# Tile addresses in multiples of 128 bytes, and the second block's first norm applied behind its projections

## The chip, the cores and the metric

The kernel runs on one core of a Trainium2 chip. The metric is the time of one execution on the device in microseconds (us); the median of three runs before the change is 2263.63 us. A core has TensorE (PE in the profile; its weight loads are listed apart as PEld), VectorE (DVE), ScalarE (ACT), GpSimd (POOL) and SyncE (SP); POOL, SP and ACT also issue DMAs here. On-chip memory (SBUF) has 128 partitions; a tile of 128x1024 fp32 takes 4096 bytes of each, and its address is the byte at which it starts in every partition.

## The reference

256 tokens of width 1024, fp32, go through two layers with PEER (a dense evaluation of 16,384 experts per layer here) and then a second block with attention, a linear recurrence (RG-LRU) and an MLP. Shortened:

```
for layer in (0, 1):                       # first block
    mix = diff_attention(x) if layer == 0 else stick_breaking(x)
    x = layer_norm(ALPHA * x + mix, ln_g[layer, 0], ln_b[layer, 0])
    x = layer_norm(ALPHA * x + peer(x), ln_g[layer, 1], ln_b[layer, 1])

u = x * rsqrt(mean(x * x, -1) + 1e-6) * attn_pre_norm        # second block
q, k, v, x_lru, g_lru, gate_attn, gate_lru = split(u @ w_in)
y_attn = moba_attention(rope(q), rope(k), v) @ w_branch_attn
y_lru = (rg_lru(conv(x_lru)) * gelu(g_lru)) @ w_branch_lru
mix = (sigmoid(gate_attn) * y_attn + sigmoid(gate_lru) * y_lru) @ w_out
h = x + rms_norm(mix)
h = h + rms_norm(square(relu(rms_norm(h) @ w_mlp_up)) @ w_mlp_down)
```

The factor of the rms norm is one number per token, so it can be taken out of the product: (r * x * gain) @ w is r * ((x * gain) @ w).

## The kernel before

Weights come as 740 tiles of 128x1024 fp32 in the order of `plan`. SyncE's queue loads them into a ring of four `raw` tiles (L50). `Stream.split` makes two fp32r tiles of each: `hi`, a cast on ScalarE (L66), and `lo = raw - hi` on VectorE (L67). Splits run two tiles ahead of the tile in use, within three pairs of `hi` and `lo`; tiles named in `keep` have buffers of their own. x is kept transposed in the same two parts, `xh` and `xl`, written by `transposed` (four TensorE transposes into PSUM, L300, then a cast, L163, and a subtraction, L164). Each product is three fp32r matmuls, high by high, high by low, low by high (L157 to L159 in `mm3`, L182 in `mm_n`).

There are two shapes of matmul. `proj_t` holds the weight tile stationary and streams 256 tokens of `xh` or `xl` (256 columns); it serves PEER's up product, the first block's q and k, the second block's x_lru, g_lru and gates, and the MLP's up product. `proj_half`, `half_pass` and `mm_n` hold 128 tokens of x (or of a hidden activation: `wh` and `wo` in PEER's down product, `uh` and `ul` in the MLP's, `mh` and `ml` in w_out) stationary and stream 512 columns of the weight tile. In a row such as `ps_h<-xh,hi` the moving operand stands first, the stationary one behind it. `ah`, `ch`, `lrr` and `laa` are activations of the second block in proj_t's role or of the recurrence's gates.

TensorE's instructions are issued in program order; while one matmul runs, the stationary operand of the next is loaded (PEld). Each engine works through its own queue in the order in which the code was written; `bg.tick()` lets background generators issue a piece of their work between tiles.

The junction from PEER to what follows: the last six weight tiles of PEER's down product are held back for the second token half (`held`, run by `finish`), so that the layer norm of the first 128 tokens (`b` = 0) runs beside them. `layer_norm` then does, per token half: the norm (`norm`, L316 to L329, on VectorE with two small ScalarE steps L266, L267 for the root), the transposes, and `half_pass(b)`, the product of this token half with the first four kept weight tiles (512 columns of the first projection). At the end of PEER 1 a pre-norm lies between norm and transposes:

```
after(b):  pre_norm(x[:, b], gain)      # before; result pnu
    squares of both halves and their sum: ACT L933 x2, DVE L935
    u[:, half] = x[:, half] * gain       # DVE L946, L948
    r = rsqrt(...)                       # ACT L266, L267, DVE L268 to L273
    u[:, :512] *= r (DVE L950); u[:, 512:] *= r (ACT L951)
```

After the junction come five calls of `proj_half` of four tiles each (the second half of q, then k and v; rope on q and k runs on VectorE behind each), then the `proj_t` products of x_lru, the two gates and, later, g_lru.

SBUF pools lie one behind another from the left and from the right; every tile is padded to a multiple of 32 bytes. Small tiles (two `eps` of 4 bytes, `gcol`, `factor`) therefore shift what follows. Addresses modulo 256, before and after (from the built programs):

```
tile                          before   after
xh, xl, jd                       128     128
raw, hi, lo (the ring's)         192     128
wh, wo (PEER down)               192     128
uh, ul (MLP down)                224       0
mh, ml (w_out)                   224       0
ah, al (branch product)           32     128
lrr, laa (recurrence gates)      224       0
x2x, x2gains (new)                 -     128
```

Full-size matmuls (fp32r, 256 or 512 columns) in the program, by the address of the moving operand less that of the next matmul's stationary operand, modulo 256:

```
columns  before                                                     after
256      192: 8294  96: 299  32: 191  others 48                     0: 8620  128: 204  64: 8
512      0: 3279  64: 473  224: 340  96: 234  128: 72  others 65    0: 3996  128: 467
```

Of the kernel before, what the change touches and what calls it, by code (L numbers as in the profile page):

```python
# [9 lines left out]
F32 = mybir.dt.float32  # L10
# [115 lines left out]
class Kernel:  # L126
    def __init__(self, tc, ctx, a):
# [85 lines left out]

    def proj_half(self, xh, xl, dst, banks="h"):
# [24 lines left out]

    def half_pass(self, b, tiles):  # L240

# [13 lines left out]
        if b:  # L255
            for i, ps in enumerate(self.passed):
                self.nc.scalar.copy(self.jd[:, i, :512], ps)
            self.passed = []
# [46 lines left out]

    def norm(self, pool, b, acc, x, g, beta):

# [18 lines left out]
        for s in halves:  # L326
            if s is halves[1]:
                centre(s)
            nc.vector.scalar_tensor_tensor(x[:, b, s], y[:, s], r, beta[:, s], ALU.mult, ALU.add)  # L329
        yield  # L330

    def layer_norm(self, pool, acc, x, g, beta, after=None):


        tiles = []
        for _ in self.norm(pool, 0, acc[0], x, g, beta):
            pass
        u0 = after(0) if after else x[:, 0]
        n1 = self.norm(pool, 1, acc[1], x, g, beta)
# [40 lines left out]
    def layer0(self, pool_x):  # L380
        nc, tc, a = self.nc, self.tc, self.a
        with ExitStack() as ctx:
# [24 lines left out]
            nc.sync.dma_start(lp.rearrange("p a b -> p (a b)"), a["lam"].unsqueeze(0).to_broadcast([P, 256]))  # L407
            gcol = one.tile([P, 1], F32, tag="gcol", name="gcol0")
            nc.sync.dma_start(gcol, a["subln"])
# [236 lines left out]
    def peer(self, layer, spill, begin):  # L646
# [212 lines left out]
        with ExitStack() as ctx:  # L859
# [58 lines left out]
            tp = ctx.enter_context(tc.tile_pool(name=f"n{layer}", bufs=1, reuse_waits="tile"))  # L918
            self.layer_norm(tp, acc, xr, gb, bb, extra(tp, xr) if extra else None)
            nc.gpsimd.dma_start(spill, xr)  # L920
# [16 lines left out]

    def pre_norm(self, pool, x, gain):

        nc = self.nc  # L940
        r = pool.tile([P, 1], F32, tag="pn_r", name=f"pnr{self.n}", bufs=2)
        u = pool.tile([P, D], F32, tag="ln_y", name=f"pnu{self.n}", bufs=2)
        halves = [slice(0, 512), slice(512, D)]
        root = self.mean_square(pool, r, [x[:, s] for s in halves], 1e-6)
        next(root)
        nc.vector.tensor_tensor(u[:, halves[0]], x[:, halves[0]], gain[:, halves[0]], ALU.mult)  # L946
        next(root)
        nc.vector.tensor_tensor(u[:, halves[1]], x[:, halves[1]], gain[:, halves[1]], ALU.mult)  # L948
        next(root)
        nc.vector.tensor_scalar(u[:, halves[0]], u[:, halves[0]], r, None, ALU.mult)  # L950
        nc.scalar.mul(u[:, halves[1]], u[:, halves[1]], r)  # L951
        return u

    def late_norm(self, pool, x, square):

        r = pool.tile([P, 1], F32, tag="lt_r", name=f"ltr{self.n}", bufs=2)
        yield from self.mean_square(pool, r, [x[:, :512], x[:, 512:]], 1e-6)
# [42 lines left out]
    def block2(self, spill):  # L1000
# [3 lines left out]
        fp = ctx_f.enter_context(tc.tile_pool(name="b2f", bufs=1))  # L1004
        factor = fp.tile([P, NB], F32, tag="factor", name="factor")
        keep = outer.enter_context(tc.tile_pool(name="b2o", bufs=1))
        with ExitStack() as ctx:
# [11 lines left out]
            nc.gpsimd.dma_start(cv, a["cols2"])  # L1019
            gb = one.tile([P, KD, 2], F32, tag="gb", name="gb2")  # L1020
# [4 lines left out]
            qk = [self.jd, kn]  # L1025
            v = keep.tile([P, NB, D], F32, tag="vh", name="v2")
            ah = one.tile([P, KD, T], F32R, tag="ah", name="ah2")
# [132 lines left out]
            def project(dst, c):  # L1160
                nc.scalar.copy(dst[:, c], self.proj_t(self.xh, self.xl))

            for dst in (qk[0], qk[1], v):
                for half in range(2):
                    if half or dst is not qk[0]:
                        self.proj_half(self.xh, self.xl, dst[:, :, half * 512 : half * 512 + 512], "acc")
                    if dst is not v:
                        rope(dst, half)
            self.bg.add(heads())
            self.bg.add(lru())  # L1170
            for half in range(2):
                ch = one.tile([P, 4, T], F32R, tag="ch", name=f"ch{half}")
                cl = one.tile([P, 4, T], F32R, tag="cl", name=f"cl{half}")
                for j in range(4):
                    c = half * 4 + j
                    o = self.proj_t(self.xh, self.xl)
                    xp = two.tile([P, T + 3], F32, tag="xp", name=f"xp{c}")
# [7 lines left out]
                    for dst in (ga, gl):  # L1185
                        nc.scalar.activation(dst[:, c], self.proj_t(self.xh, self.xl), AF.Tanh, scale=0.5)
                        if dst is ga:
# [31 lines left out]
            self.bg.drain()  # L1219
            xp = outer.enter_context(tc.tile_pool(name="b2x", bufs=1, side="right"))  # L1220
            x = xp.tile([P, NB, D], F32, tag="x", name="x2")
            nc.gpsimd.dma_start(x, spill)
            gains = self.gains(xp, "gains", a["attn_post_norm_2"][0], a["mlp_pre_norm_2"][0])
            mh = keep.tile([P, KD, T], F32R, tag="vh", name="mh2")
# [68 lines left out]
def body(tc, a, stop="all"):  # L1293
    nc = tc.nc
    with ExitStack() as ctx:
# [18 lines left out]
        def begin(pool, late):  # L1314
            (pre,) = k.gains(pool, "pre", a["attn_pre_norm_2"][0], late=late)
            return lambda temps, x: lambda b: k.pre_norm(temps, x[:, b], pre)

# [87 lines left out]
```

## Time and profile before

| | |
|---|---|
| median of 3 runs | 2263.63 us (2262.33 to 2263.73) |
| profiled execution | 2266.94 us |
| its span | 2265.1 us |
| mean granted TensorE clock | 0.994 |

All rows shown come from this one profiled execution. A row of the timeline has the start in us from the span's start, the duration, engine, line, operation, out<-in, shapes, the count of merged instructions and, in brackets, the idle time before it with what ended it. A row of the windows has the stretch, its length, for each engine the busy time and the number of instructions, the granted clock (1.00 is full speed), the share of the DMA engines and GB/s. A matmul's duration overlaps its successors' (0.28 us for 256 columns, 0.39 for 512, while a new one starts every 0.11 or 0.23 us), so pace is read from starts or from counts.

### The profile page before, as it was taken

What the parts mean: (1) busy time and instruction counts of PE and PEld (TensorE: products, weight loads), DVE (VectorE), ACT (ScalarE), POOL (GpSimd) and SP (SyncE); (2) the same over time, 40 slices, a digit from 0 to 9 for tenths busy, and PEclk for the clock granted to TensorE, in tenths of its full rate; (3) what the DMA queues carried; (4) which work ended last, traced back from release to release, by engine and by line L of the source; (5) the groups of instructions that cost most, each with busy time, mean ns of one, the idle gap of its engine ahead of it and who ended that gap; (6) DMA issues with size and microseconds to landing.
All of it is one profiled execution on the core that took longest, in us unless ns stands there. A gap on an engine that the chain in (4) does not pass through costs nothing.

```text
span 2265.1 us, 39924 instructions
## 1 busy us (share of the span) xinstructions
PE 2218.6 (98%) x15028; PEld 2002.1 (88%) x15028; DVE 1757.5 (78%) x3501; ACT 1229.2 (54%) x2115; POOL 54.8 (2%) x118
## 2 busy tenths in 40 slices
PE   8999999999999999999999999999999899999998
PEld 7779999999888887988999999988888789997986
DVE  6879998887776668677999888777666857886754
ACT  5744455666544554674445566644554546655643
POOL 4200000000000000000000000000000000000000
PEclk9999999999999999999999999999999999999999
DMA  7556676557777777545666655777777655555664
GB/s 247 160 175 230 218 233 228 195 202 239 253 242 242 243 238 248 191 138 178 224 226 233 221 199 194 264 243 243 239 244 258 211 176 165 177 175 179 214 187 139
DMA packets 151954, 481.96 MB, mean 213 GB/s; under 512 B 17888, under 2 KB 18944, under 8 KB 150480
## 3 DMA queue, kind: packets, MB, share of 16 engines
q1 hardware_dynamic: 126576, 423.09, 58.2%
q10 hardware_dynamic: 19008, 34.61, 4.1%
q0 software_dynamic: 6176, 21.70, 2.7%
q8 instruction: 118, 1.93, 0.3%
q14 instruction: 76, 0.62, 0.1%
HBM read 437.39 MB, written 39.85 MB: 211 GB/s over the span
## 4 chain that ended last, share of the span: by engine, by line
PE 84%; DVE 6%; issue 4%; ACT 3%; DMA 3%; POOL 0%; ACTq 0%; DVEq 0%; SPq 0%; POOLq 0%
PE ps_acc L182 31%; PE ps_h L157 15%; PE ps_h L159 15%; PE ps_h L158 15%; DVE lo L67 1%; PE ps_acc L821 1%; PE ps_acc L822 1%; PE ps_acc L158 1%; PE ps_acc L157 1%; PE ps_acc L159 1%; ACT hi L66 1%; PE ps_acc L705 0%; DMA raw<-peer_w_q 0%; DMA raw<-peer_v 0%; DVE lns L319 0%
## 5 line engine op out<-in xcount | busy, mean ns | idle before, releaser
L67 DVE TENSOR_TENSOR lo<-raw,hi 128x1024 fp32r<-128x1024 f32 x740 | 901.5, 1222 | 414.3 <-ACT hi L66 410.8
L66 ACT CAST hi<-raw 128x1024 fp32r<-128x1024 f32 x740 | 774.6, 1050 | 432.6 <-issue 288.0
L157 PE MATMUL ps_h<-xh,hi 128*128 128x256 f32 x2784 | 789.9, 284 | 0.8 <-ACT k L628 0.8
L159 PE MATMUL ps_h<-xh,lo 128*128 128x256 f32 x2784 | 774.5, 278 | 3.4 <-DVE lo L67 3.3
L158 PE MATMUL ps_h<-xl,hi 128*128 128x256 f32 x2784 | 774.4, 278 | 0.0
L157 PEld LDWEIGHTS ps_h<-xh,hi 128*128 128x128 f32 x2784 | 526.3, 189 | 5.9 <-issue 1.7
L159 PEld LDWEIGHTS ps_h<-xh,lo 128*128 128x128 f32 x2784 | 525.1, 189 | 4.2 <-DVE lo L67 4.2
L158 PEld LDWEIGHTS ps_h<-xl,hi 128*128 128x128 f32 x2784 | 524.7, 188 | 0.2
L182 PE MATMUL ps_acc<-hi,wh 128*128 128x512 f32 x1024 | 317.9, 390 | 0.1
L182 PE MATMUL ps_acc<-hi,wo 128*128 128x512 f32 x1024 | 318.0, 390 | 0.0
L182 PE MATMUL ps_acc<-lo,wh 128*128 128x512 f32 x1024 | 317.4, 389 | 0.2 <-DVE lo L67 0.2
L848 ACT ACTIVATE hs<-ps_h 128x256 f32<-128x256 f32 x254 | 97.6, 384 | 341.0 <-PE ps_h L159 171.6
L182 PEld LDWEIGHTS ps_acc<-hi,wh 128*128 128x128 f32 x1024 | 191.6, 188 | 41.8 <-ACT wh L163 2.4
L182 PEld LDWEIGHTS ps_acc<-hi,wo 128*128 128x128 f32 x1024 | 191.8, 188 | 41.1 <-DVE wo L164 1.6
L182 PEld LDWEIGHTS ps_acc<-lo,wh 128*128 128x128 f32 x1024 | 192.1, 188 | 40.5 <-DVE lo L67 0.7
L874 DVE TENSOR_TENSOR jd<-G,jd 128x256 f32<-128x256 f32 x256 | 106.9, 418 | 3.3 <-ACT G L824 3.3
L164 DVE TENSOR_TENSOR wo<-jd,wh 128x256 fp32r<-128x256 f32 x256 | 107.2, 419 | 2.0 <-ACT wh L163 2.0
L163 ACT CAST wh<-jd 128x256 fp32r<-128x256 f32 x256 | 101.7, 397 | 10.0 <-DVE jd L874 9.8
L824 ACT ACTIVATE G<-ps_acc 128x64 f32<-128x64 f32 (+1 forms) x256 | 81.9, 385 | 7.4 <-issue 1.5
L157 PE MATMUL ps_h<-hi,xh 128*128 128x512 f32 x160 | 68.4, 428 | 9.0 <-ACT hi L66 8.0
L821 PE MATMUL ps_acc<-oh 128*128 128x128 f16 x512 | 69.4, 221 | 0.0
L822 PE MATMUL ps_acc<-oh 128*128 128x128 f16 x512 | 68.3, 219 | 0.0
(359 smaller groups left out, 2372.7 us busy)
## 6 DMA issues: line engine op xcount, KB each, us to landing
raw<-peer_u SPq DMA_DIRECT2D x256, 512.0 KB, 4.5
raw<-peer_v SPq DMA_DIRECT2D x256, 512.0 KB, 4.3
jd<-H ACTq DMA_DIRECT2D x128, 256.0 KB, 4.2
H<-hs SPq DMA_DIRECT2D x126, 256.0 KB, 2.1
raw<-w_in SPq DMA_DIRECT2D x32, 512.0 KB, 3.7
raw<-w_up SPq DMA_DIRECT2D x32, 512.0 KB, 4.0
raw<-w_down SPq DMA_DIRECT2D x32, 512.0 KB, 3.7
raw<-w_qkv SPq DMA_DIRECT2D x24, 512.0 KB, 4.4
```

What stands on the lines that cost most here:

```text
L66: self.nc.scalar.copy(hi, raw)
L67: self.nc.vector.tensor_sub(lo, raw, hi)
L157: mm(out, lh, rh, start=start, stop=False)
L158: mm(out, lh, rl, start=False, stop=False)
L159: mm(out, ll, rh, start=False, stop=stop)
L163: self.nc.scalar.copy(hi, src)
L164: self.nc.vector.tensor_sub(lo, src, hi)
L182: mm(acc[half], x, w[:, half * 512 : half * 512 + 512], start=a, stop=b)
L821: mm(out, o[:, 0, j], o[:, 1, j], start=True, stop=False)
L822: mm(out, o[:, 0, j], o[:, 2, j], start=False, stop=True)
L848: nc.scalar.activation(hs[i // 2][:, i % 2], o, AF.Gelu)
L874: nc.vector.tensor_tensor(w, g[:, i - first], hl[i // 2][:, i % 2], ALU.mult)
```

## The change

Two things in one diff.

Pads. `factor` and `gcol` are widened to 128 and 64 bytes, `gb` to 128; two unused tiles, of 64 bytes behind the constants on the left and 96 on the right, bring what follows to multiples of 128 bytes (table above). No instruction belongs to this.

The late factor. `pre_norm` is gone. `norm` takes a function `then` that multiplies each half of x by the gain, into the norm's own buffer `lny`, directly behind the norm of that half (L355), and the transposes read it. The rms factor of each token half is computed by `late_factor` (squares, sum and root as before) into `self.factor`, and enters where products leave PSUM with tokens on partitions: in `half_pass` (L268) and `proj_half` (L237), as a multiply on ScalarE in place of the copy. The `proj_t` products have tokens along the free dimension, so x is rescaled for them: the factor goes through DRAM (`rd`) and comes back spread over all partitions (`rb`), and the background generator `rescale` does `xz = (xh + xl) * rb` and splits it into `x2`, a pair of k at a time, over eight ticks that begin after eleven. `x2` takes 16 KB on the right, later reused for `x` and `gains`.

```diff
+        self.factor = c.tile([P, 32], F32, tag="factor", name="fac")[:, :NB]
         self.ident = c.tile([P, P], F32, tag="ident", name="ident")
+        pads = {"left": 64, "right": 96}
+        c.tile([P, pads["left"] // 4], F32, tag="pad", name="padl")
+        top = ctx.enter_context(tc.tile_pool(name="top", bufs=1, side="right"))
+        top.tile([P, pads["right"] // 4], F32, tag="pad", name="padr")
...
     def proj_half(self, xh, xl, dst, banks="h", by=None):
-            self.nc.scalar.copy(dst[:, b], acc[b])
+            if by is None:
+                self.nc.scalar.copy(dst[:, b], acc[b])
+            else:
+                self.nc.scalar.mul(dst[:, b], acc[b], by[:, b : b + 1])
...
     def norm(self, pool, b, acc, x, g, beta, then=None):
             nc.vector.scalar_tensor_tensor(x[:, b, s], y[:, s], r, beta[:, s], ALU.mult, ALU.add)
+            if then:
+                then(y, s)
...
+    def layer_norm(self, pool, acc, x, g, beta, gain=None):
+            def scaled(b):
+                def then(y, s):
+                    u[b] = y
+                    nc.vector.tensor_tensor(y[:, s], x[:, b, s], gain[:, s], ALU.mult)
+                return then
+            factors = [self.late_factor(pool, x[:, b], self.factor[:, b : b + 1]) for b in range(NB)]
...
         for h in range(2):
             next(n1)
-            self.transposed(0, h, u0)
+            self.transposed(0, h, u[0])
         self.st.split(self.st.used + NJ, self.st.used)
+        if factors:
+            next(factors[0])
         next(n1)
         self.half_pass(0, tiles)
-        u1 = after(1) if after else x[:, 1]
         for h in range(2):
-            self.transposed(1, h, u1)
-        self.half_pass(1, tiles)
+            self.transposed(1, h, u[1])
+        if factors:
+            next(factors[1])
+            for f in factors:
+                for _ in f:
+                    pass
+        self.half_pass(1, tiles, self.factor if factors else None)
...
+    def late_factor(self, pool, x, r):
+        yield from self.mean_square(pool, r, [x[:, :512], x[:, 512:]], 1e-6)
...
+            x2 = [rx.tile([P, KD, T], F32R, tag=t, name="x2" + t) for t in ("x", "gains")]
+            nc.gpsimd.dma_start(rd.rearrange("b p -> p b"), self.factor)
+            nc.gpsimd.dma_start(rb, rd.rearrange("b p -> (b p)").unsqueeze(0).to_broadcast([P, T]))
+            def rescale():
+                for _ in range(11):
+                    yield
+                for k in range(0, KD, 2):
+                    s = slice(k, k + 2)
+                    z = two.tile([P, 2, T], F32, tag="m2", name=f"xz{k}")
+                    nc.vector.tensor_tensor(z, self.xh[:, s].bitcast(F32), self.xl[:, s].bitcast(F32), ALU.add)
+                    yield
+                    nc.vector.tensor_tensor(z, z, rb.unsqueeze(1).to_broadcast([P, 2, T]), ALU.mult)
+                    self.part(x2[0][:, s], x2[1][:, s], z)
+                    yield
...
-                        self.proj_half(self.xh, self.xl, dst[:, :, half * 512 : half * 512 + 512], "acc")
+                        self.proj_half(self.xh, self.xl, dst[:, :, half * 512 : half * 512 + 512], "acc", self.factor)
-                    o = self.proj_t(self.xh, self.xl)
+                    o = self.proj_t(*x2)
```

TensorE's order keeps its 15,708 rows; only names change. On VectorE, the norm of the first 128 tokens at the end of PEER 1 (`xr` is the normed x, `pnu` before and `lny` after what the transposes read), before:

```order
L329 SCALAR_TENSOR_TENSOR xr_19679<-lny_21198,lnr_21201,gains_20816 128x512
L323 SCALAR_TENSOR_TENSOR lny_21198<-lny_21198,lnm_21200,gains_20816 128x512
L329 SCALAR_TENSOR_TENSOR xr_19679<-lny_21198,lnr_21201,gains_20816 128x512
L946 TENSOR_TENSOR pnu_21221<-xr_19679,gains_20817 128x512
L935 TENSOR_TENSOR mss_21223<-mss_21223 128x1
L268 TENSOR_SCALAR rsx_21228<-mss_21223 128x1
L948 TENSOR_TENSOR pnu_21221<-xr_19679,gains_20817 128x512
L270 SCALAR_TENSOR_TENSOR rsz_21230<-rsy_21229,rsx_21228 128x1
L271 TENSOR_SCALAR rsz_21230<-rsz_21230 128x1
L273 TENSOR_TENSOR pnr_21220<-rsy_21229,rsz_21230 128x1
L950 TENSOR_SCALAR pnu_21221<-pnu_21221,pnr_21220 128x512
L316 SCALAR_TENSOR_TENSOR lny_21240<-xr_19679,ps_acc_18173 128x512
```

The same place after:

```order
L340 SCALAR_TENSOR_TENSOR xr_19685<-lny_21204,lnr_21207,gains_20822 128x512
L355 TENSOR_TENSOR lny_21204<-xr_19685,gains_20823 128x512
L334 SCALAR_TENSOR_TENSOR lny_21204<-lny_21204,lnm_21206,gains_20822 128x512
L340 SCALAR_TENSOR_TENSOR xr_19685<-lny_21204,lnr_21207,gains_20822 128x512
L355 TENSOR_TENSOR lny_21204<-xr_19685,gains_20823 128x512
L327 SCALAR_TENSOR_TENSOR lny_21228<-xr_19685,ps_acc_18179 128x512
```

The sum, the root and the scaling have left this place; the two multiplies by the gain stand behind their halves, and the second token half's norm (L327) follows at once.

On ScalarE, from the last copies of the second token half into xh (`ps_m`) to the next weight tiles, before:

```order
L951 ACTIVATE pnu_21308<-pnu_21308,pnr_21307 128x512
L163 CAST xh<-ps_m_21327 128x4x128
L163 CAST xh<-ps_m_21334 128x4x128
L66 CAST hi_21348<-raw_21283 128x1024
L66 CAST hi_21358<-raw_21291 128x1024
L66 CAST hi_21368<-raw_21299 128x1024
L257 COPY jd<-ps_h_21276 128x512
```

And after (`msj` squares, `rsy` the root's two steps, `fac` the factor):

```order
L168 CAST xh<-ps_m_21301 128x4x128
L168 CAST xh<-ps_m_21308 128x4x128
L964 ACTIVATE msj_21315,mss_21316<-xr_19685 128x512 x2
L277 ACTIVATE rsy_21321<-mss_21249,eps1e-06_76 128x1
L278 ACTIVATE rsy_21321<-rsy_21321 128x1
L277 ACTIVATE rsy_21331<-mss_21316,eps1e-06_76 128x1
L278 ACTIVATE rsy_21331<-rsy_21331 128x1
L66 CAST hi_21346<-raw_21277 128x1024
L66 CAST hi_21356<-raw_21285 128x1024
L66 CAST hi_21366<-raw_21293 128x1024
L268 ACTIVATE jd<-ps_h_21270,fac 128x512
```

The second token half's squares and the roots of both halves now stand between those copies and the split of the next three weight tiles.

On VectorE, in the v projection, the splits of four consecutive tiles (before) have the rescale between them (after):

```order
L67 TENSOR_TENSOR lo_21736<-raw_21691,hi_21735 128x1024
L67 TENSOR_TENSOR lo_21754<-raw_21733,hi_21753 128x1024
L67 TENSOR_TENSOR lo_21772<-raw_21751,hi_21771 128x1024
L67 TENSOR_TENSOR lo_21790<-raw_21769,hi_21789 128x1024
L67 TENSOR_TENSOR lo_21812<-raw_21787,hi_21811 128x1024
```

```order
L67 TENSOR_TENSOR lo_21745<-raw_21698,hi_21744 128x1024
L1060 TENSOR_TENSOR xz_21718<-xz_21718,rb 128x512
L169 TENSOR_TENSOR x2gains<-xz_21718,x2x 128x512
L67 TENSOR_TENSOR lo_21766<-raw_21742,hi_21765 128x1024
L1058 TENSOR_TENSOR xz_21781<-xh,xl 128x512
L67 TENSOR_TENSOR lo_21786<-raw_21763,hi_21785 128x1024
L1060 TENSOR_TENSOR xz_21781<-xz_21781,rb 128x512
L169 TENSOR_TENSOR x2gains<-xz_21781,x2x 128x512
```

Three more VectorE instructions per two tiles stand among the splits, until four pairs of k are done. GpSimd's queue gets the two DMAs of the factor behind that of `mask` and ahead of the memsets of `xp`.

More of the change, by code (lines that the diff above doesn't have):

```diff
@@ L238, in junction, with half_pass @@
         return ctx
-    def half_pass(self, b, tiles):
+    def half_pass(self, b, tiles, by=None):
         acc = self.ps("h")
@@ L304, in transposed, with norm @@
         self.part(xh[sl], xl[sl], v)
-    def norm(self, pool, b, acc, x, g, beta):
+    def norm(self, pool, b, acc, x, g, beta, then=None):
         nc = self.nc
@@ L329, in norm @@
             nc.vector.scalar_tensor_tensor(x[:, b, s], y[:, s], r, beta[:, s], ALU.mult, ALU.add)
+            if then:
+                then(y, s)
         yield
-    def layer_norm(self, pool, acc, x, g, beta, after=None):
-        tiles = []
-        for _ in self.norm(pool, 0, acc[0], x, g, beta):
-            pass
-        u0 = after(0) if after else x[:, 0]
-        n1 = self.norm(pool, 1, acc[1], x, g, beta)
+    def layer_norm(self, pool, acc, x, g, beta, gain=None):
+        nc, tiles, factors = self.nc, [], []
+        if gain is not None:
+            u = [None] * NB
+            def scaled(b):
[4 more added lines that the diff above has]
+            factors = [self.late_factor(pool, x[:, b], self.factor[:, b : b + 1]) for b in range(NB)]
+        else:
+            u, scaled = [x[:, b] for b in range(NB)], lambda b: None
+        for _ in self.norm(pool, 0, acc[0], x, g, beta, scaled(0)):
+            pass
+        n1 = self.norm(pool, 1, acc[1], x, g, beta, scaled(1))
         for h in range(2):
             next(n1)
-            self.transposed(0, h, u0)
+            self.transposed(0, h, u[0])
         self.st.split(self.st.used + NJ, self.st.used)
+        if factors:
+            next(factors[0])
         next(n1)
         self.half_pass(0, tiles)
-        u1 = after(1) if after else x[:, 1]
         for h in range(2):
-            self.transposed(1, h, u1)
-        self.half_pass(1, tiles)
+            self.transposed(1, h, u[1])
[5 more added lines that the diff above has]
+        self.half_pass(1, tiles, self.factor if factors else None)
     def plan(self):
@@ L407, in layer0 @@
             nc.sync.dma_start(lp.rearrange("p a b -> p (a b)"), a["lam"].unsqueeze(0).to_broadcast([P, 256]))
-            gcol = one.tile([P, 1], F32, tag="gcol", name="gcol0")
+            gcol = one.tile([P, 16], F32, tag="gcol", name="gcol0")[:, :1]
             nc.sync.dma_start(gcol, a["subln"])
@@ L936, in mean_square @@
         yield from self.rsqrt(pool, out, ss[:, 0:1], eps, 1.0 / D, by)
[L938 to L952, printed above, removed]
     def late_norm(self, pool, x, square):
         r = pool.tile([P, 1], F32, tag="lt_r", name=f"ltr{self.n}", bufs=2)
-        yield from self.mean_square(pool, r, [x[:, :512], x[:, 512:]], 1e-6)
+        yield from self.late_factor(pool, x, r)
         self.nc.vector.tensor_tensor(square, r, r, ALU.mult)
         yield
+    def late_factor(self, pool, x, r):
+        yield from self.mean_square(pool, r, [x[:, :512], x[:, 512:]], 1e-6)
     def post_norm(self, pool, acc, x, gain, out=None, by=None, then=None):
@@ L1004, in block2 @@
         fp = ctx_f.enter_context(tc.tile_pool(name="b2f", bufs=1))
-        factor = fp.tile([P, NB], F32, tag="factor", name="factor")
+        factor = fp.tile([P, 32], F32, tag="factor", name="factor")[:, :NB]
         keep = outer.enter_context(tc.tile_pool(name="b2o", bufs=1))
@@ L1019, in block2 @@
             nc.gpsimd.dma_start(cv, a["cols2"])
-            gb = one.tile([P, KD, 2], F32, tag="gb", name="gb2")
+            gb = one.tile([P, KD, 4], F32, tag="gb", name="gb2")
             nc.gpsimd.tensor_scalar(gb[:, :, 0:1], cv[:, :, 5:6], -1.0, None, ALU.mult)
@@ L1025, in block2 @@
             qk = [self.jd, kn]
+            rx = outer.enter_context(tc.tile_pool(name="b2x", bufs=1, side="right"))
+            x2 = [rx.tile([P, KD, T], F32R, tag=t, name="x2" + t) for t in ("x", "gains")]
+            rd = self.dram.tile([NB, P], F32, tag="rd", name="rd")
+            rb = two.tile([P, 2, T], F32, tag="th", name="rb")[:, 0]
+            nc.gpsimd.dma_start(rd.rearrange("b p -> p b"), self.factor)
[11 more added lines that the diff above has]
+                    yield
             v = keep.tile([P, NB, D], F32, tag="vh", name="v2")
@@ L1160, in project @@
             def project(dst, c):
-                nc.scalar.copy(dst[:, c], self.proj_t(self.xh, self.xl))
+                nc.scalar.copy(dst[:, c], self.proj_t(*x2))
+            self.bg.add(rescale())
             for dst in (qk[0], qk[1], v):
```

19 lines of the change are left out of this document (11 added, 8 removed).

## The prediction

> **What bounds the kernel now.** I read the page first (busy time, chain, groups), then TensorE's busy time by windows, then the timeline of TensorE, VectorE and ScalarE around the start of the second block.
>
> ```profile
> span 2265.1 us, 39924 instructions
> ...
> PE 2218.6 (98%) x15028; PEld 2002.1 (88%) x15028; DVE 1757.5 (78%) x3501; ACT 1229.2 (54%) x2115; POOL 54.8 (2%) x118
> ...
> PE 84%; DVE 6%; issue 4%; ACT 3%; DMA 3%; POOL 0%; ACTq 0%; DVEq 0%; SPq 0%; POOLq 0%
> ...
> L67 DVE TENSOR_TENSOR lo<-raw,hi 128x1024 fp32r<-128x1024 f32 x740 | 901.5, 1222 | 414.3 <-ACT hi L66 410.8
> L66 ACT CAST hi<-raw 128x1024 fp32r<-128x1024 f32 x740 | 774.6, 1050 | 432.6 <-issue 288.0
> ```
>
> TensorE is the bound: 98% busy, 84% of the chain. Only two things can shorten this program: matmuls that follow each other faster, or one of TensorE's 46 us of gaps. The change touches both.
>
> Pace of the matmuls. In the view by windows (length, busy time, instructions, granted clock, DMA) TensorE is never idle in these rows, so length over count is the pace. A count includes what is in flight at an edge: about 2.5 too many for 256 columns, 1.7 for 512.
>
> ```profile
> core 0: us, PE busy (x), PEclk, DMA share, GB/s
> 24.00:38.00 14.00, 14.00 (x126) 1.00 0.74 219
> 278.00:329.00 51.00, 51.00 (x433) 1.00 0.69 231
> 1174.00:1225.00 51.00, 51.00 (x435) 1.00 0.68 229
> 2098.00:2168.00 70.00, 70.00 (x597) 1.00 0.67 209
> 620.00:700.00 80.00, 80.00 (x355) 1.00 0.78 243
> 1825.00:1865.00 40.00, 40.00 (x177) 1.00 0.63 191
> 2062.00:2070.00 8.00, 8.00 (x36) 1.00 0.77 265
> 2170.00:2235.00 65.00, 65.00 (x280) 1.00 0.62 191
> 2016.00:2032.00 16.00, 16.00 (x137) 1.00 0.71 210
> 2035.00:2045.00 10.00, 10.00 (x88) 1.00 0.64 195
> ```
>
> All at clock 1.00, and yet equal matmuls differ. With 256 columns: 14 / 123.5 = 113.4 ns in the first row, 51 / 430.5 = 118.5, 51 / 432.5 = 117.9 and 70 / 594.5 = 117.7 in the next three, with the same kind of operands. With 512: 80 / 353.3 = 226.4 ns in PEER's down product, 40 / 175.3 = 228.2 in q, k, v, 8 / 34.3 = 233 in w_out, 65 / 278.3 = 233.6 in the MLP's down product. The last two rows (a 256-column product from ah, and lrr and laa) give 118.9 and 117.0. What differs is where the operands lie. While one matmul streams its moving operand, the next one's stationary operand is loaded (PEld, 88% busy); the difference of those two addresses (table in the kernel's description), modulo 256 bytes, sorts the rows: 0 for PEER's down product (226.4), 64 for q, k, v, 128 for w_out, 224 for the MLP's down product, 96 and 32 for the last two, and 192 for all matmuls of 256 columns on xh and xl, which keep one of two paces, 113.4 or 117.8, for long stretches.
>
> **The pads.** They put raw, hi, lo at 128 modulo 256, where xh, xl, jd lie already: the difference becomes 0 for 8,620 of 8,832 matmuls of 256 columns and 3,996 of 4,463 of 512. I take 113.33 and 226.67 ns as the undisturbed pace and add what each spacing in the trace lies above it, group by group (spacings over 9% longer are waits and left out): 256 columns at 192, 11.2 us; at 96, 1.2; at 32, 0.6; 512 columns at 224, 2.25 (312 x 6.9 ns gives 2.15); at 64 and 96, 2.4; at 128 and 160, 0.7; at 0, 0.45: 18.8 us. As a cross-check the three slow rows of 256 columns alone hold 51 - 430.5 x 0.11333 = 2.2, 2.0 and 2.6 us, or 6.8.
>
> What stays: the MLP's down product goes from 224 to 128, where w_out's 233 ns says 1.8 of its 2.25 stays; w_out and the attention outputs 0.7; lrr, laa 0.6; half of the half passes' 2.4, which are changes of stage; 0.45 at 0. And where VectorE is full, a faster TensorE waits for lo:
>
> ```profile
> core 0: us, PE busy (x) PEld busy (x) DVE busy (x) ACT busy (x) POOL busy (x), PEclk, DMA share, GB/s
> 200.00:300.00 100.00, 100.00 (x872) 98.75 (x871) 96.65 (x308) 46.41 (x73) 0.00 (x0) 1.00 0.67 227
> 2000.00:2025.00 25.00, 25.00 (x211) 24.98 (x211) 24.80 (x36) 14.22 (x20) 0.00 (x0) 1.00 0.63 191
> ```
>
> 200 to 300 has 3.3% to give, more than the 1.8 us asked; 2000 to 2025 has 0.2 us, so about 0.8 stays there. 18.8 - 1.8 - 0.7 - 0.6 - 1.2 - 0.45 - 0.8 = 13.2; I take **-13**. No row shows 256 columns at difference 0, so both ends are open: at best all 18.8 go; at worst 0 is the bad place for 256 columns and all 8,832 run at 117.8: 8,832 x 4.5 ns = 39.7, less the 13.0 paid now, +26.7. I take the first because the one group at 0, PEER's down product, is the one without excess.
>
> The Trainium skill speaks against all of this: "TensorE: Matmul & The Clock Gate", Part 2, step 1 (LDWEIGHTS), says that TensorE has two independent read ports and that loading the next weights takes no read bandwidth from the running matmul. By that rule pads are worth 0 and only the junction below moves the time, to about 2257.5. The rows disagree as to the pace (226.4 against 233.6 ns for one instruction at one clock), but that the address is the cause is my reading.
>
> **The junction to the second block.** TensorE's last deferred matmul of PEER, and what follows:
>
> ```profile
> 1795.69 0.39 PE L182 MATMUL ps_acc<-hi,wo 128*128 128x512 f32 x1
> ...
> 1799.07 1.56 PE L300 MATMUL ps_m<-ident,pnu 128*128 128x128 f32 x8 [2.98 <-DVE pnu L950]
> ...
> 1810.32 1.94 PE L300 MATMUL ps_m<-ident,pnu 128*128 128x128 f32 x8 [2.88 <-DVE pnu L950]
> ...
> 1819.83 0.40 PE L157 MATMUL ps_acc<-hi,xh 128*128 128x512 f32 x1
> ```
>
> 24.14 us from the last matmul to the projections' first, with two waits for the scaled pnu and, after each, a slow clock:
>
> ```profile
> 1799.50:1803.00 3.50, 3.50 (x13) 2.75 (x11) 2.68 (x6) 1.17 (x2) 0.00 (x0) 0.51 0.00 0
> 1809.70:1816.60 6.90, 6.28 (x19) 5.07 (x20) 4.59 (x6) 5.20 (x7) 0.00 (x0) 0.51 0.32 100
> 1938.00:1945.00 7.00, 5.42 (x45) 5.15 (x44) 6.32 (x15) 5.41 (x13) 1.28 (x4) 1.00 0.47 140
> 2070.00:2077.00 7.00, 4.55 (x18) 3.37 (x17) 5.23 (x10) 2.72 (x8) 0.00 (x0) 0.76 0.18 69
> 1820.00:1870.00 50.00, 50.00 (x220) 40.98 (x220) 28.30 (x65) 23.20 (x27) 2.74 (x8) 1.00 0.59 184
> ```
>
> Half clock for 3.5 and 6.9 us loses about 5.2 us. The same code without a pre-norm stands at the first PEER's end, so it prices the junction:
>
> ```profile
> 899.97 0.39 PE L182 MATMUL ps_acc<-hi,wo 128*128 128x512 f32 x1
> 900.20 1.13 PE L300 MATMUL ps_m<-ident,xr 128*128 128x128 f32 x8
> ...
> 914.67 0.28 PE L157 MATMUL ps_h<-xh,hi 128*128 128x256 f32 x1
> ...
> 904.81 0.30 ACT L266 ACTIVATE rsy<-lnm,eps1e-05_74 128x1 f32<-128x1 f32 x1 [2.85 <-DVE lnm L320]
> ...
> 909.18 0.59 ACT L163 CAST xh<-ps_m 128x512 fp32r<-128x512 f32 x1 [0.52 <-PE ps_m L300]
> ```
>
> 14.70 us, at full clock. What the new code has beyond it, by the rows of before:
>
> ```profile
> 1796.11 0.68 DVE L946 TENSOR_TENSOR pnu<-xr,gains 128x512 f32<-128x512 f32 x1
> ...
> 1798.33 0.16 DVE L273 TENSOR_TENSOR pnr<-rsy,rsz 128x1 f32<-128x1 f32 x1
> 1798.53 0.48 DVE L950 TENSOR_SCALAR pnu<-pnu,pnr 128x512 f32<-128x512 f32 x1
> ...
> 1794.77 0.63 ACT L933 ACTIVATE msj<-xr 128x512 f32<-128x512 f32 x1 [1.61 <-DVE xr L329]
> 1795.31 0.19 ACT L933 ACTIVATION_READ_ACCUMULATOR msj<-xr 128x1 f32 x1
> ...
> 1797.23 0.29 ACT L266 ACTIVATE rsy<-mss,eps1e-06_76 128x1 f32<-128x1 f32 x1 [0.23 <-DVE mss L935]
> 1797.56 0.20 ACT L267 ACTIVATE rsy<-rsy 128x1 f32<-128x1 f32 x1
> ```
>
> (a) Four multiplies of 128x512 by the gain, on VectorE's chain from norm to norm to transposes: 4 x 0.65 = 2.6 us. (b) The first token block's squares, 2 x 0.73 on ScalarE, stand ahead of the second norm's L266 (L277 after), where ScalarE idled 2.85 us: free. (c) The second block's squares and both factor chains stand after the last xh cast and ahead of the next tile's hi: 1.46 + 0.53 + 0.95 (L267's end to L273's end, and the next sum) + 0.53 = 3.5 us. In the first junction that cast ends at 909.77 and the half pass 4.9 us later. So hi ends 3.5 + 1.05 = 4.55 and lo 4.55 + 1.22 = 5.8 us after the cast, while the second matmul wants lo at 5.1: a stall of 0.65 us, new. L950 and L951 go. Sum: 14.70 + 2.6 + 0.65 = 17.95 against 24.14: **-6.2**. Ends: -9.4 if (a) and (c) hide, -2.8 if both stretches' worth of one 6.9 us half clock (3.4 us) stays.
>
> **The rescale and the rest.** Four pairs of add, multiply and subtract of 128x512 on VectorE, 12 x 0.68 = 8.2 us, in eight tiles of 2.7 us, about 22 us. The window 1820 to 1870 shows VectorE 57% busy, so it goes to 0.57 + 8.2 / 22 = 94% while rope runs and less beside v, where each pair of tiles needs 2 x 1.22 + 2.05 = 4.5 of 5.4 us; splits run two tiles ahead. ScalarE's four casts and the scaled evacuations meet 46% busy. Cover gone, a late lo or x2 would cost up to 2 us; a gain is excluded, since nothing is removed there. I take +0.3. The two DMAs that spread the factor stand behind the mask in GpSimd's queue, ahead of memsets wanted 50 us later; their result is wanted 11 tiles (30 us) on: 0, and if they took longer than those 30 us the queue of VectorE would hold up lo behind the multiply. Nothing is moved past SyncE's queue.
>
> Sum: -13 - 6.2 + 0.3 = -18.9. The profiled execution is 2266.94 (span 2265.1 and 1.8 around it), so 2248.0 for it; it stands 3.3 above the median of 2263.63, which gives **2244.7**.
>
> **Rivals.**
> 1. Pads do nothing (the two paces have another cause, say the clock's phase or the DMA): 2263.6 - 6.2 + 0.3 = 2257.7. For it: 256 columns at one difference, 192, run at two paces. Against: each 512-column group keeps one pace, in its own place. 0.16.
> 2. The late norm brings little: gaps of about 0.6 and 1.6 us remain before the transposes, since u of the second block still waits for two norms. A gap of 1.58 us lies in the window 1938 to 1945, at full clock; one of 2.08 in 2070 to 2077, at 0.76. If it halves the clock, 3.4 us come back, and with 2 for the rescale: 2244.7 + 3.4 + 1.7 = 2249.8. 0.09. The Trainium skill's same page, Part 1, "What's actually happening", has the clock judged in free-running windows of about 3.4 us, so that phase decides; the 3.5 us stretch agrees.
> 3. Slower: difference 0 is where the two reads of 256-column matmuls meet, and the slow pace becomes permanent: +26.7 - 2.5 (512 columns) - 6.2 + 0.3 = +18, 2282. It decides once over about half of the 8,832 run at 117.8 (20 us above nothing). For it: 192 also shows long fast stretches, so a fixed 0 could freeze the wrong pace. Against: 226.4 at 0. 0.06.
> 4. In between, part of 1 with 3, within 4.5 us of before: 0.03.
>
> My forecast has 0.66, by itself 2238 to 2251. A measurement tells this kernel from no change at about 0.2%, 4.5 us (the three runs spread 1.4). The range 2236 to 2259 holds the forecast and rivals 1 and 2, its low end near 18.8 + 9.4 gone; left out are 3, 4 and tails. Faster 0.91, same 0.03, slower 0.06.
>
> **What would show it.** Right: the MLP's up product and the stages of 278 and 1174 at 113.4 ns throughout; q, k, v at 226.7; the MLP's down product still near 232; no slow clock at the junction, about 18 us from L182 to the first projection matmul, with a wait of 0.65 for lo L67 at the start; no TensorE wait in the v projection. Wrong: stretches at 117.8 at unchanged or larger share (1 or 3); 0.5 clock behind the transposes (2).

## The result: slower by 1.5%

The changed kernel takes 2294.44 us in the median (2292.04 to 2302.12), the kernel before 2263.68 beside it: ratio 1.0147, interval 1.0131 to 1.0163, where 0.992 was forecast. That is the third rival, "difference 0 is where the two reads meet", and dearer than priced there. The page of the kernel after:

```profile
span 2292.4 us, 39938 instructions
...
PE 2251.8 (98%) x15028; PEld 2037.6 (89%) x15028; DVE 1768.9 (77%) x3511; ACT 1230.5 (54%) x2117; POOL 58.0 (3%) x120
...
PE 87%; DVE 4%; issue 4%; DMA 2%; ACT 2%; POOL 0%; DVEq 0%; SPq 0%; POOLq 0%; ACTq 0%
```

TensorE has the same 15,028 matmuls in the record and is busy 33.2 us longer: the loss is in the pace of matmuls, not in a wait. Its windows, in the same columns as before (a count includes the matmuls in flight at the edges, 2.4 too many for 256 columns, 1.7 for 512):

```profile
24.00:38.00 14.00, 14.00 (x119) 1.00 0.74 198
278.00:329.00 51.00, 51.00 (x428) 1.00 0.66 223
620.00:700.00 80.00, 80.00 (x355) 1.00 0.77 243
1850.00:1890.00 40.00, 40.00 (x178) 1.00 0.76 206
2115.00:2195.00 80.00, 80.00 (x670) 1.00 0.62 196
2197.00:2260.00 63.00, 63.00 (x273) 1.00 0.64 191
```

256 columns (rows 1, 2, 5): 14 / 116.6 = 120.1, 51 / 425.6 = 119.8 and 80 / 667.6 = 119.8 ns. There are no fast stretches any more; even the start of the program, 113.4 before, is at 120. There all 117 starts stand 120 ns apart, although VectorE is busy for only 9.1 and ScalarE for 6.6 of the 14 us: the slow pace does not come and go with the work of these two engines. 512 columns: PEER's down product at 0 is still 226.4 and q, k, v, now at 0, go from 228.2 to 40 / 176.3 = 226.9; the MLP's down product, moved from 224 to 128, gives 63 / 271.3 = 232.2, as the row of w_out had said. Summed over all spacings, what lies above the undisturbed pace is 59.1 us against 19.8, so +39.3; waits (spacings over 9% long) are 51.0 against 63.4, so -12.4. Together +26.9, and the span grew by 27.3.

The junction did what was forecast. TensorE's timeline, and all engines in the windows of the junction and of q, k, v:

```profile
1827.85 0.39 PE L187 MATMUL ps_acc<-hi,wo 128*128 128x512 f32 x1
...
1829.83 0.66 PE L311 MATMUL ps_m<-ident,lny 128*128 128x128 f32 x4 [1.14 <-DVE lny L355]
...
1836.63 0.63 PE L311 MATMUL ps_m<-ident,lny 128*128 128x128 f32 x4 [0.31 <-DVE lny L355]
1838.80 0.63 PE L311 MATMUL ps_m<-ident,lny 128*128 128x128 f32 x4 [1.55 <-DVE lny L355]
...
1844.75 0.39 PE L162 MATMUL ps_acc<-hi,xh 128*128 128x512 f32 x1
1845.38 0.50 PE L163 MATMUL ps_acc<-lo,xh 128*128 128x512 f32 x1 [0.23 <-DVE lo L67]
```

```profile
1828.00:1845.00 17.00, 13.92 (x67) 10.53 (x64) 14.02 (x33) 8.30 (x21) 0.54 (x1) 1.00 0.15 62
1845.00:1899.00 54.00, 53.77 (x237) 44.41 (x237) 39.00 (x81) 28.47 (x35) 5.92 (x10) 1.00 0.72 203
```

16.90 us from the last held matmul to the first of the projections, where it was 24.14; gaps of 0.3 to 1.6 us leave the clock at 1.00, and the new wait for lo is there, 0.23 us long.

### The profile page after: what moved, and what is told of

The parts are those of the page before. It is cut to its first block, busy times and chain, and to the rows that moved or that the text cites. A ratio compares the mean times of both kernels' runs of the same rounds, so it can differ in the third digit from the quotient of the medians.

```text
span 2292.4 us, 39938 instructions
## 1 busy us (share of the span) xinstructions
PE 2251.8 (98%) x15028; PEld 2037.6 (89%) x15028; DVE 1768.9 (77%) x3511; ACT 1230.5 (54%) x2117; POOL 58.0 (3%) x120
## 4 chain that ended last, share of the span: by engine, by line
PE 87%; DVE 4%; issue 4%; DMA 2%; ACT 2%; POOL 0%; DVEq 0%; SPq 0%; POOLq 0%; ACTq 0%
PE ps_acc L187 31%; PE ps_h L162 16%; PE ps_h L164 15%; PE ps_h L163 15%; PE ps_acc L852 1%; PE ps_acc L853 1%; PE ps_acc L163 1%; PE ps_acc L164 1%; PE ps_acc L162 1%; DVE lo L67 1%; ACT hi L66 1%; PE ps_acc L736 0%; DVE rr L1153 0%; DMA raw<-peer_w_q 0%; DVE lny L327 0%
## 5 line engine op out<-in xcount | busy, mean ns | idle before, releaser
L162 PE MATMUL ps_h<-xh,hi 128*128 128x256 f32 x2528 | 728.2, 288 | 0.9 <-ACT k L659 0.9
L163 PE MATMUL ps_h<-xl,hi 128*128 128x256 f32 x2528 | 714.4, 283 | 0.0
L164 PE MATMUL ps_h<-xh,lo 128*128 128x256 f32 x2528 | 714.3, 283 | 0.0
L162 PEld LDWEIGHTS ps_h<-xh,hi 128*128 128x128 f32 x2528 | 483.8, 191 | 5.9 <-issue 1.7
L163 PEld LDWEIGHTS ps_h<-xl,hi 128*128 128x128 f32 x2528 | 484.2, 192 | 0.1
L164 PEld LDWEIGHTS ps_h<-xh,lo 128*128 128x128 f32 x2528 | 483.9, 191 | 0.0
L164 PE MATMUL ps_h<-x2x,lo 128*128 128x256 f32 x256 | 73.3, 286 | 2.5 <-DVE lo L67 2.5
L162 PE MATMUL ps_h<-x2x,hi 128*128 128x256 f32 x256 | 74.5, 291 | 0.0
```

The costliest lines, as they stand in the source:

```text
L162: mm(out, lh, rh, start=start, stop=False)
L163: mm(out, lh, rl, start=False, stop=False)
L164: mm(out, ll, rh, start=False, stop=stop)
```

## The experiments

The theory after this result (A): with 256 columns, the pace is set by the difference, modulo 256 bytes, between the moving operand's address and that of the next stationary operand; 0 is a bad value and 192, where the kernel before stood, a good one. In the ratios below each kernel stands against the kernel before, run beside it on the same chip; those medians were 2259.9 to 2262.5.

**Which half of the change.** The first kernel is the kernel before with the addresses of the change (the three widened tiles, an empty tile in the place of the new factor, and the two pads) and nothing else; the second has the late factor and the old widths:

```diff
-        self.factor = c.tile([P, 32], F32, tag="factor", name="fac")[:, :NB]
+        self.factor = c.tile([P, NB], F32, tag="factor", name="fac")
-        pads = {"left": 64, "right": 96}
+        pads = {"left": 224}       # 32 + 224 = 256: no address on the left moves modulo 256
...
-        top.tile([P, pads["right"] // 4], F32, tag="pad", name="padr")
```

> The pads of the change without its late factor: pre-norm and order of the kernel before, addresses of the kernel after. Theory A (the difference between the moving operand's address and that of the next stationary operand, modulo 256, sets the pace of matmuls of 256 columns; 0 is its bad value): they start every 119.9 ns as after, in all stages, and the junction takes 24.1 us as before, so about 2294 + 7 = 2301 us. Theory B (the late factor and the new x2 cause the loss, the pads are worth nothing): paces as before, 2264 us. Theory C (the slow pace comes from something else that varies between builds): between the two, with 256-column stages at mixed paces.

> The late factor without the pads: the small tiles have their old widths and the constants grow by 256 bytes, so every address on the left is as before modulo 256 (xh less hi is 192). Theory A: 256-column matmuls keep their two paces of 113.4 and 117.8 ns, the junction takes 17 us, so 2264 - 7 = 2257 us (2254 to 2260). Theory B: about 2294 us. The matmuls on x2 stand at difference 32 here, where lrr and laa had 1.03 times the undisturbed pace.

Pads alone: 2301.0 us, 1.0178 (1.0161 to 1.0195), and A forecast 2301. That the two agree so closely is partly luck, since the kernel before ran 3.8 us faster here (2259.91) than beside the change (2263.68). Its rows for the start of the program and for the stretch of 278 to 329:

```profile
24.00:38.00 14.00, 14.00 (x119) 1.00 0.72 215
278.00:329.00 51.00, 51.00 (x429) 1.00 0.66 227
```

The late factor alone: 2260.52 us, 0.9998 (0.9988 to 1.0008). The junction takes 17.6 us there, but the 7 us did not come out at the end; see below.

**Difference or alignment.** 64 bytes ahead of xh move everything on the left together; a longer left pad moves hi, lo and what lies behind them against xh and xl.

```diff
+        c.tile([P, 16], F32, tag="pad0", name="pad0")          # third: common shift
         self.xh = c.tile([P, KD, T], F32R, tag="xh", name="xh")
...
-        pads = {"left": 64, "right": 96}
+        pads = {"left": 192, "right": 96}                      # fourth: 128 more
```

> The kernel after with 64 bytes put in front of xh: everything on the left moves by 64 bytes, so tiles lie at 64 modulo 128 while all differences on the left stay 0. Theory A: still 119.9 ns, about 2293 us (x2, on the right, changes to difference 192 and may gain up to 5 us). Theory D (what hurts is that tiles start at multiples of 128 bytes, not the difference): paces as before, about 2257 us.

> The kernel after with the left pad 128 bytes longer: hi and lo, and what lies behind them, move against xh and xl. 256-column matmuls stand at difference 128, q, k, v of 512 columns too; PEER's down product stays at 0. Theory A: the pace leaves 119.9 ns; if 128 acts on 256 columns as on 512 (half the loss there, 2.5%), about 2270 us; if it is free, 2246 us. Theory D: tiles still start at multiples of 128 bytes, so 119.9 ns and 2294 us.

Common shift: 2298.53 us, 1.0166 (1.0147 to 1.0186), 5 us above the forecast. Difference 128: 2290.29, 1.0128 (1.0111 to 1.0145). The stretch of 278 to 329 in the one and the other:

```profile
278.00:329.00 51.00, 51.00 (x428) 1.00 0.66 231
```

```profile
278.00:329.00 51.00, 51.00 (x433) 1.00 0.65 221
```

All left addresses moved by 64 and the pace stayed at 119.8 ns; the difference moved and it left (51 / 430.6 = 118.4). So the difference counts, not the alignment (theory D falls). But 128 is hardly better than 0: of the two values in the forecast, 2270 and 2246, neither came.

**The rest of the curve.** Left pads of 0, 160 and 96 bytes in the kernel after:

> The kernel after without its left pad: xh less hi becomes 64 modulo 256 (x2 the same), q, k, v of 512 columns stand at 192. Theory F (the two reads meet by the distance of their addresses in either direction): like 192, 1.01 times the undisturbed pace, 8295 matmuls less 0.047 x 113.3 ns each, 44 us below after: about 2250 us. Theory G (the load runs behind the stream, so that only a stationary operand ahead of the moving one, 192, stays clear): 1.03 to 1.05, 2270 to 2290 us.

> The kernel after with the left pad 96 bytes longer: xh less hi is 160 modulo 256, q, k, v at 96. Theory F: like 96 (ah had 1.04 to 1.05): about 2280 us. Theory G: between 128 (1.05) and 192 (1.01): 1.03, about 2268 us.

> The kernel after with the left pad 32 bytes longer: xh less hi is 224 modulo 256, q, k, v at 32. Theory F: like 32 (lrr, laa and the x2 of the second experiment had 1.03 to 1.035): about 2270 us. Theory G: between 192 (1.01) and 0 (1.057): 1.03, about 2268 us. Neither theory tells the two apart here; the run is for the curve.

2281.78 (1.0091, 1.0074 to 1.0108), 2286.04 (1.0122, 1.0105 to 1.0139) and 2286.72 us (1.0125, 1.0107 to 1.0142). Theory F, which takes distance in either direction, falls: 64 is not like 192. Theory G forecast the first of the three rightly and missed the other two by 18 us, so neither theory gives the curve. The means over all spacings of a group (waits left out), from the profiles of all kernels, relative to 113.33 and 226.67 ns:

```
difference    0       32      64      96      128     160     192            224
256 columns   1.057   1.035   1.037   1.047   1.050   1.044   1.006 to 1.015 1.044
512 columns   1.001   1.029   1.012   1.030   1.025   1.031   1.029          1.029
```

For 256 columns 192 is the only good place of the eight, for 512 columns 0 is. The kernel before had most of each there. The values at 192 average stretches of two paces (see below). The table says what the pace goes with, not why.

**Which pair.** The kernel before with 192 bytes between the hi and lo tiles, so that on xh and xl only matmuls followed by a load of lo change, to 0:

```diff
+            if not i:
+                pool.tile([P, 48], F32, tag="mid", name="mid", bufs=1)
             lo = pool.tile([P, 1024], F32R, tag="lo" + n, name=f"lo{i}")
```

> The kernel before with 192 bytes between the hi and the lo tiles of the ring: lo, and what lies behind it, moves; xh, xl and hi stay. In proj_t the three matmuls of a k are L157 (own stationary hi, next hi), L158 (own hi, next lo) and L159 (own lo, next hi). Theory A (the moving operand against the next stationary operand): xl less lo is 0, so L158 alone goes to 119.9 ns, while L157 and L159 keep the pace of 192 (113.3 to 117.8). Rival (a matmul against its own stationary operand): L159 alone is slow. Second rival (any tile at a bad place slows the whole sequence): all three at 117 to 120. By theory A and the curve so far the loss is 2784 x 5.1 ns = 14 us there and 6 in PEER's down product (hi less wh becomes 64): about 2280 us.

2309.8 us, 1.0213 (1.0197 to 1.0229), where 2280 was expected. TensorE's timeline in the stretch of q and k (L159 to L161 stand for L157 to L159):

```profile
290.25 0.28 PE L159 MATMUL ps_h<-xh,hi 128*128 128x256 f32 x1
290.37 0.29 PE L160 MATMUL ps_h<-xl,hi 128*128 128x256 f32 x1
290.50 0.28 PE L161 MATMUL ps_h<-xh,lo 128*128 128x256 f32 x1
290.62 0.28 PE L159 MATMUL ps_h<-xh,hi 128*128 128x256 f32 x1
290.74 0.29 PE L160 MATMUL ps_h<-xl,hi 128*128 128x256 f32 x1
```

In full resolution the starts are 122, 127 and 118 ns apart: L160, the one followed by lo, is the slowest and L161, whose own stationary operand is lo, the fastest. Over the whole program the means of L159, L160 and L161 are 118.7, 120.0 and 117.7 ns. So the first rival, by which the matmul on lo alone is slow, falls. But theory A's forecast that L159 and L161 keep the pace of 192 did not come either, and the second rival's (all three at 117 to 120) did. The order of the three speaks for the pair "moving, next stationary"; the experiment does not isolate that pair, because a bad pair also costs its neighbours. The curve therefore holds for sequences in which all differences agree.

The sum, which charged L158 alone, was 29 us short. Of the 49 us some 33 lie on the matmuls of xh and xl, where 14 were charged, and 14.5 in PEER's down product, where 6 were: its mean spacing went from 226.8 to 231.5 ns, with differences of 0 and 64 mixed, so q, k, v's 1.012 for 64 did not carry over to it. Another 1.6 us lie in q, k, v.

**The late factor's missing 7 us.** In the second experiment q, k, v took 57.7 us instead of 54.9, with TensorE waiting 1.8 us in the midst for hi and lo. All engines, 9 us of that stage, and the row of the factor's write:

```profile
1822.00:1831.00 9.00, 9.00 (x41) 7.38 (x40) 4.97 (x15) 2.89 (x4) 0.71 (x3) 1.00 0.79 34
```

```profile
rd<-fac POOLq DMA_DIRECT2D x1, 1.0 KB, 8.5
```

The DMA engines are 79% busy and move 34 GB/s: the write, 256 elements of 4 bytes issued at 1820.4, takes 8.5 us to land and weight loads crawl meanwhile; the read back (`rb`) is issued only at 1829.2. The time of q, k, v beside such a write varies: it took 10.2 us in the kernel after, where q, k, v still took 54.9, and 7.6 us in the third experiment, where they took 59.0. The fifth experiment spreads the factor with two matmuls:

```diff
-            nc.gpsimd.dma_start(rd.rearrange("b p -> p b"), self.factor)
-            nc.gpsimd.dma_start(rb, rd.rearrange("b p -> (b p)").unsqueeze(0).to_broadcast([P, T]))
...
+                for b in range(NB):                  # in rescale, after six ticks
+                    mm(wide[:, b * P : b * P + P], self.factor[:, b : b + 1].to_broadcast([P, P]), self.ident, start=True, stop=True)
+                nc.scalar.copy(rb, wide[:, :T])
```

> The late factor at the old addresses (as the second experiment), with the factor spread over the partitions by two small fp32 matmuls into PSUM and a copy, in place of the two DMAs through DRAM. Theory H (the scattered write of the factor, 256 elements of 4 bytes, holds up the weight loads behind it for some 8 us; that is why q, k, v took 57.7 us in the second experiment instead of 54.9): q, k, v take 54.9 us plus about 0.5 for the matmuls, no wait for hi there, DMA at 150 GB/s or more in every slice but the ones where it already paused before; the time is 2.5 to 3 us below the second experiment's, about 2257.5 where the kernel before has 2260. Rival (the rescale's VectorE work or the changed order of splits holds up hi): 57.7 us as in the second experiment, no gain.

> The fifth experiment's kernel once more (late factor by matmuls, old addresses, x2 at 32) in five rounds. Theory J: the gain of 6 us less 2.7 for x2 at 32, 0.9985 of before, within the interval of the fifth experiment. Rival K: 1.000 to 1.001.

The same stretch of that kernel, from the same point of the stage:

```profile
1823.40:1832.40 9.00, 9.00 (x41) 7.40 (x40) 5.60 (x16) 5.16 (x6) 0.86 (x4) 1.00 0.72 256
```

256 GB/s and no wait of TensorE for another engine: q, k, v take 55.8 us, theory H holds in the profile. In time it does not show: 2260.21 us, 0.9996 (0.9986 to 1.0007), and again 2261.93, 0.9994 (0.9985 to 1.0003), where H forecast 2257.5 and J 0.9985.

**The pace at 192 wanders.** The kernel before, unchanged, profiled in another execution:

> The kernel before, unchanged, profiled once more. Theory A': at difference 192 the pace is not set by the address alone: each stretch falls on 113.4 or 117.8 ns by how the engines happen to be timed, so the stretches of 278 to 329 and 1174 to 1225 may change their pace between two executions of one program, and the sum above the undisturbed pace differs by a few us (about 16 to 24). Rival (the pace is fixed by the program): the same stretches are slow again, 19.8 us in all.

2260.37 us, span 2258.5, against 2265.1 in the profile that the prediction read. The two stretches that were slow there:

```profile
278.00:329.00 51.00, 50.77 (x447) 1.00 0.70 238
1174.00:1225.00 51.00, 50.57 (x443) 1.00 0.69 232
```

447 and 443 matmuls instead of 433 and 435: they fell on the fast pace. Above the undisturbed pace stand 17.3 us instead of 19.8. So the same stretch of the same program can take either pace at 192 in different executions, and a few us of difference between two single profiles prove nothing.

The starts show one thing more. In the profile that the prediction read, xh and xl have 182 uninterrupted stretches of at least 15 matmuls: 164 keep 113.3 ns to their end, 18 keep 117.8, and none changes on the way. There the pace is taken at the start of a stretch and changes only across an interruption.

**Everything in its place.** The fifth experiment's kernel with each group of operands moved to the lowest point of the curve, and the kernel before with pads for the same differences:

```diff
-        factor = fp.tile([P, NB], F32, tag="factor", name="factor")
+        factor = fp.tile([P, 64], F32, tag="factor", name="factor")[:, :NB]     # uh, ul to 0 from hi
...
+        top.tile([P, 24], F32, tag="pad", name="padr")                          # x2 to 192
...
+            one.tile([P, 48], F32, tag="pado", name="pado2")                    # lrr, laa to 192
...
+            one.tile([P, 16], F32, tag="pada", name="pada2")                    # ah, al, ch, cl to 192
```

In the kernel before the last pad has 192 bytes, since `cos` keeps its place there.

> The late factor with matmuls for its spread (as the fifth experiment), with pads that put each operand where the curve is lowest: xh, x2, ah, ch, lrr, laa at 192 from hi (256 columns), uh, ul, most of mh, ml at 0 (512 columns), q, k, v at 64; cos of the second block moves into the constants, which takes the place of part of a pad. Theory A: excess above the undisturbed pace 15 us against 20 in the kernel before and 22 in the fifth experiment; with 7 us from the junction and 1 back in q, k, v, about 11 below before: 2249 us where before has 2260 (2246 to 2253, since the pace at 192 varies). Rival (only the pairs of xh and hi matter, the small groups are noise): as the fifth experiment, within 0.1% of before.

> The kernel before, with its pre-norm, and pads alone that put the operands at the same differences as in the tenth experiment (8,783 matmuls of 256 columns at 192, 3,847 of 512 at 0). Against the next kernel it leaves only the late factor. Theory J (the late factor is worth the 7 us of the junction less about 1 in q, k, v wherever the addresses are good): about 2255 us where before has 2260.8, 6 above the placed kernel with the late factor. Rival K (the late factor is worth nothing in timed runs, as the second and fifth experiments suggest with 0.9998 and 0.9996, and the whole gain of the tenth is placement): about 2249.5, the same as the placed kernel.

> The tenth experiment's kernel once more, beside the one above on the same chip. Theories J and K: 0.995 of before, about 2249.5 where before has 2260.8; its profile may differ by 2 or 3 us from the tenth's by the two paces at 192.

The placed kernel: 2249.57 us, 0.9952 (0.9939 to 0.9966), and again, on another chip, 2254.25, 0.9965 (0.9951 to 0.9978): 0.35 to 0.5% faster than the kernel before, about 2% faster than the change. Its profile, the page's first line and the MLP's up and down products:

```profile
span 2245.1 us, 39945 instructions
```

```profile
2073.00:2150.00 77.00, 77.00 (x679) 1.00 0.69 211
2152.00:2235.00 83.00, 83.00 (x368) 1.00 0.57 172
```

77 / 676.6 = 113.8 ns and 83 / 366.3 = 226.6, where the kernel before had 117.7 and 233.6. 10.5 us stand above the undisturbed pace, in the fastest of its five timed executions. The down product gained by its move from 224 to 0. The up product stood at 192 before and stands there now, so the curve does not explain its gain. Nor does chance from execution to execution: it runs at 117.8 ns in all five profiles of the kernel before and of the late factor at the old addresses, and at 113.3 for most of its length in all three with these pads. In the built programs its differences are the same but for two matmuls of 768, which stood at 160 before; whether these two set the pace of what follows was not tested.

The kernel before with the same differences takes 2261.11 us, 0.9993 (0.9984 to 1.0002), where J forecast 2255 and K 2249.5. The two placed kernels differ by the late factor, 6.9 us (0.9965 against 0.9993, so 0.28% with some 0.16 either way): that is J's difference, and K, by which the late factor is worth nothing, falls. Placement by itself is worth 0.07% in timed runs, which is not clear of zero, though that kernel's one profile shows 11.4 us above the pace instead of 17 to 20: its eleven times run from 2254.18, the profiled one, to 2263.35.

## Why the prediction was wrong, point by point

- **The bound**, TensorE's pace and gaps, was right, and so was the reading of the rows: the address difference sorts the paces. The experiments bore out that reading. By the Trainium skill's rule on two independent read ports ("TensorE: Matmul & The Clock Gate", Part 2, step 1) the pace would not depend on it. The table above, 1.001 to 1.057 at one clock, disagrees; that the two reads are what meets is the likeliest reading, and not shown by itself.
- **The pads, -13: the step that failed.** The text said "No row shows 256 columns at difference 0" and then took the good end "because the one group at 0, PEER's down product, is the one without excess". That group has 512 columns, and the curve of 512 does not carry over: its good place is the worst one of 256. The term came out at +39.3, with a start every 120 ns. The bad end given, +26.7, was too small as well: it priced 117.8 ns as the worst pace, while ah's row, 118.9, stood in the same fence; 119.8 was measured. What the trace did hold was that 192, the kernel's own place, was already good: 113.4 in long stretches.
- **What stays**: the MLP's down product at 128 (232.2 ns, w_out's 233 said so) and q, k, v at 0 (226.9) were right; the 512 columns alone did gain.
- **The junction, -6.2**: 24.14 to 16.90 us, -7.2, priced by the first PEER's end plus four multiplies. The stall for lo was 0.23 in place of 0.65. No clock was halved: after gaps of 0.3 to 1.6 us it stayed at 1.00, so rival 2 did not occur.
- **The rescale, +0.3**: about right in the kernel after, where q, k, v took 54.9 us against 54.4 with the pads alone. But "take longer than those 30 us" looked at the wrong danger: the factor's scattered write is itself what delays the weight loads, and it cost 2.8 us in the second experiment.
- **Rivals**: the third had the right place, a bad 0 for 256 columns, and the sign, at 0.06 and 2282. Between two open ends 45 us apart (-18.8 and +26.7), with no row at that width, its chance should have been near that of the forecast.

What stays open: why a difference of 192 has two paces and what picks one at the start of a stretch; and why the late factor at the old addresses shows 0.02 to 0.06% in timed runs while its profiles have -7.2 at the junction, +0.9 in q, k, v and +1.7 for x2 at 32 (2.7 us above the pace there, about 1 by the rate of 192). The fifth experiment's sum, -4.6, or 0.20%, lies beyond its intervals (the second's, -6.5 + 2.8 + 1.7, is -2.0 and agrees). The wandering pace can fill the gap: in the two profiles of the fifth kernel xh and xl stand 12.4 and 12.9 us above the undisturbed pace over 7,584 matmuls, in the two of the kernel before 11.9 and 9.4 over 8,352, which is 10.8 and 8.5 for as many. That takes 1.6 to 4.4 us off the sum and brings it inside the intervals; that it is so in every execution was not shown.

## What to carry to other kernels

A change of a few bytes in a small tile can move a whole program by over 1% when TensorE is the bound, so compare addresses before and after, modulo 256, for the moving operand and the next stationary one, and do it by width: a good place for 512 columns says nothing of 256. Before padding for alignment's sake, read the pace by stage from windows and keep the place that already runs fast; then move the others towards it. A price that no row shows for that shape deserves even odds, not the sign of the nearest row.

## What the runs showed of the hardware

- With fp32r operands the pace of back-to-back matmuls goes with the difference, modulo 256 bytes, between the address of the moving operand and that of the next stationary one: 113.3 to 119.8 ns on the mean for 256 columns, 226.7 to 233.7 for 512, at a granted clock of 1.00. Moving both by 64 bytes left 119.8 ns at 119.8. A bad pair slows its neighbours too (122, 127 and 118 ns for one pair in three).
- One place, 192 modulo 256 with 256 columns, has two paces, and the same stretch of the same program takes the one or the other in different executions (433 or 447 matmuls in 51 us). An uninterrupted stretch keeps its pace to the end (164 at 113.3 ns, 18 at 117.8, none mixed, in one profile).
- A write of 256 elements of 4 bytes to DRAM took 7.6 to 10.2 us to land. In the second experiment the DMA engines were shown 79% busy meanwhile and moved 34 GB/s in all.
